# Residual stream with the tokens on the partitions in a four-layer pool, MLA, NA, pool backbone

## The chip, the cores and the metric

The kernel runs on one core of a Trainium2 chip. The metric is the device time of one execution in microseconds (us). A core has TensorE (PE; its weight loads are a row of their own, PEld), VectorE (DVE), ScalarE (ACT), GpSimd (POOL) and SyncE (SP), which here issues DMAs.

## The reference, cut to what matters

Two streams, 256 latent tokens `x` and 256 context tokens `ctx`, have 1024 channels and pass four layers. A layer has a token mixer (pool, MLA, NA, pool) and a SwiGLU FFN of 2816 hidden channels. Shift, scale and gate of each half come from `silu(c) @ ada_w[i]` (1024 by 6144, fp32, one map of weights for both streams).

```
for i in range(4):
    h = rmsnorm(x, norm_g[i, 0]) * (1 + sc_m) + sh_m
    x = x + g_m * rmsnorm(mixer(h), norm_g[i, 1])
    h = rmsnorm(x, norm_g[i, 2]) * (1 + sc_f) + sh_f
    x = x + g_f * rmsnorm((silu(h @ wg) * (h @ wu)) @ w_down, norm_g[i, 3])
```

The context does the same in layers 0 and 1 with its own shift, scale and gate. In layer 2 it only gives keys and values, and layer 3 has the latent tokens alone. The pool mixer takes, for four groups of 256 channels, the mean over a centred window of 2, 4, 8 or 16 tokens less the token itself, times a 256 by 256 matrix for each group and a scale for each channel.

## The kernel before, in words

Every value that goes into a large product is split into two fp32r parts, hi and lo, and a product is three matmuls: hi hi, hi lo, lo hi (`mm3`, L332 to L337). Weights come from DRAM as chunks of eight 128 by 128 tiles (512 KB, five `raw` slots). ACT makes hi (L157), DVE makes lo (L161), five chunks of each are kept, and each chunk is used once.

The residual stream `xs` has channels on the partitions: eight tiles of 128 channels by 512 tokens, latent tokens first. In all products the weights are stationary and the tokens move, 512 columns where both streams pass (layers 0 and 1) and 256 where the latent tokens pass alone. An output product (`ffn_down`, `Wo.rest`) makes one tile of 128 output channels after another. Since a norm runs over the channels, its sums go across partitions: for each tile `y_stats` (L495 to L512) makes squares and a product on ACT and DVE, POOL adds them to a running sum (L512), and at the end PE sums over the partitions (L526), ACT and DVE make the factors, and PE spreads them (L551). DVE and POOL then add to x (`post`, L571, L573), and `renorm` (L600, L589, L591) makes the two parts of the next h, tile by tile.

What lies between two sub-layers is called an edge here: from the first matmul of an output product's last part to the end of `head` (L910 to L913), which multiplies h with the first four column tiles of the next weights as h comes. The order in an edge is written by hand, one letter a step (`ORDERS`, read by `Edge.run`). With both streams the last four column tiles are made for the latent tokens first and for the context (`quanta`) while the latent h is made. The letters p and q prepare weights, the letter a is a step of the adaLN maps on PE: four fp32 matmuls with one 512 KB chunk of `ada_w` (L379), of which a unit (one of six of a layer) has eight. All other adaLN steps are done by DVE in the FFNs (L395).

The first layer's pool mixer (`start`) takes window sums with DVE and POOL adds along the tokens; the last layer's (`pool`) multiplies with a 256 by 256 band matrix for each group. `Closing` ends the program: transposes of x and of the gated y, the norm, and four stores.

## Time and profile before

| | us |
|---|---|
| median of 3 runs (1777.34 to 1782.39) | 1780.4 |
| span of the profiled execution, first to last instruction | 1779.5 |
| PE busy | 1676.0 |
| DVE busy | 1177.7 |
| ACT busy | 726.8 |
| POOL busy | 248.4 |

The profile gives the profiled execution's span and no device time of its own for it; the span lies within the range of the three runs. A share of busy time is a mean over stages. The matmuls' ends are modelled and overlap, so a busy PE says little by itself; the distance from one matmul's start to the next is what counts.

### The profile page before, as it was taken

To read this page: it belongs to the slowest core of one execution; us is meant where nothing else is said; L and a number is where in the kernel's file an instruction comes from. 1 tells how busy PE (TensorE), PEld (TensorE's weight loads), DVE (VectorE), ACT (ScalarE), POOL (GpSimd) and SP (SyncE) were. 2 spreads that over 40 slices of the span, in tenths; PEclk is the share of its full clock that TensorE was granted. 3 is DMA by queue.
4 is the path that set the end of the run, shared out by engine and by line. 5 is a ranking of instruction groups with operands and counts; after the bars stand their busy time and mean duration, and the time that the engine had idled before them with its cause. 6 is when DMAs were issued, how large, how long until landed. Compare 5 with 4: busy or idle time off the path is not lost.

```text
span 1779.5 us, 27077 instructions
## 1 busy us (share of the span) xinstructions
PE 1676.0 (94%) x10726; PEld 1453.7 (82%) x10726; DVE 1177.7 (66%) x1833; ACT 726.8 (41%) x1264; POOL 248.4 (14%) x199
## 2 busy tenths in 40 slices
PE   4789999999999999899999999899989999989998
...
GB/s 303 288 184 219 170 197 172 156 175 160 48 99 43 43 123 56 48 211 180 191 176 168 176 154 55 127 91 114 114 131 203 304 285 190 190 93 203 181 186 73
DMA packets 82270, 279.45 MB, mean 157 GB/s; under 512 B 9312, under 2 KB 16224, under 8 KB 82144
## 3 DMA queue, kind: packets, MB, share of 16 engines
...
q8 instruction: 84, 1.38, 0.3%
q10 hardware_dynamic: 1568, 0.86, 0.2%
...
HBM read 276.65 MB, written 1.05 MB: 156 GB/s over the span
## 4 chain that ended last, share of the span: by engine, by line
PE 82%; DVE 11%; ACT 4%; issue 1%; DMA 1%; POOL 0%; ACTq 0%; DVEq 0%; POOLq 0%
PE acc L335 21%; PE acc L336 21%; PE acc L337 21%; PE acc L913 2%; PE acc L910 2%; PE acc L911 2%; PE adp L379 2%; PE aux L335 2%; DVE wl L161 2%; PE aux L336 2%; PE aux L337 1%; DMA raw<-in_ada_w 1%; DVE yq L507 1%; DVE rh L591 1%; PE aux L1484 1%
## 5 line engine op out<-in xcount | busy, mean ns | idle before, releaser
L161 DVE TENSOR_TENSOR wl<-raw,wh 128x1024 fp32r<-128x1024 f32 x323 | 408.5, 1271 | 218.6 <-ACT wh L157 215.6
L335 PE MATMUL acc<-rh,wh 128*128 128x256 f32 (+1 forms) x1392 | 468.9, 337 | 0.0
L336 PE MATMUL acc<-rh,wh 128*128 128x256 f32 (+1 forms) x1392 | 465.3, 334 | 2.3 <-DVE rh L350 2.3
L337 PE MATMUL acc<-rh,wl 128*128 128x256 f32 (+1 forms) x1392 | 465.0, 334 | 0.0
L157 ACT ACTIVATE wh<-raw 128x1024 fp32r<-128x1024 f32 x323 | 337.1, 1051 | 237.9 <-PE acc L336 121.0
L512 POOL TENSOR_TENSOR ya<-ya,yq 128x768 f32<-128x768 f32 x71 | 146.6, 2070 | 1081.3 <-DVE yq L507 715.2
L335 PEld LDWEIGHTS acc<-rh,wh 128*128 128x128 f32 x1392 | 265.2, 191 | 34.4 <-issue 7.4
L336 PEld LDWEIGHTS acc<-rh,wh 128*128 128x128 f32 x1392 | 265.4, 191 | 27.5 <-DVE rh L350 2.5
L337 PEld LDWEIGHTS acc<-rh,wl 128*128 128x128 f32 x1392 | 265.2, 191 | 26.3 <-DVE wl L161 0.2
L335 PE MATMUL acc<-rx,wh 128*128 128x256 f32 (+1 forms) x816 | 260.8, 320 | 0.0
L337 PE MATMUL acc<-rx,wl 128*128 128x256 f32 (+1 forms) x816 | 259.1, 318 | 0.0
L336 PE MATMUL acc<-rx,wh 128*128 128x256 f32 (+1 forms) x816 | 259.1, 317 | 0.0
L395 DVE SCALAR_TENSOR_TENSOR ff_a<-raw,sc,ff_a 128x1024 f32<-128x1024 f32 x154 | 192.1, 1278 | 0.6 <-DMA raw<-in_ada_w 0.3
L335 PEld LDWEIGHTS acc<-rx,wh 128*128 128x128 f32 x816 | 154.5, 189 | 12.0 <-issue 0.8
L337 PEld LDWEIGHTS acc<-rx,wl 128*128 128x128 f32 x816 | 154.4, 189 | 11.3
L336 PEld LDWEIGHTS acc<-rx,wh 128*128 128x128 f32 x816 | 154.6, 189 | 11.1
L364 ACT ACTIVATE rx<-big 128x512 fp32r<-128x512 f32 (+1 forms) x80 | 42.0, 525 | 247.3 <-DVE big L681 247.3
L681 DVE TENSOR_TENSOR big<-big,acc 128x512 f32<-128x512 f32 (+1 forms) x88 | 48.6, 552 | 112.4 <-PE acc L337 107.8
L910 PE MATMUL acc<-rh,wh 128*128 128x256 f32 x304 | 85.9, 310 | 8.0 <-ACT rh L589 6.8
L589 ACT ACTIVATE rh<-t,m 128x256 fp32r<-128x256 f32 x88 | 44.9, 510 | 108.5 <-DVE t L600 108.4
L911 PE MATMUL acc<-rh,wl 128*128 128x256 f32 x304 | 83.3, 301 | 0.0
L350 DVE TENSOR_TENSOR rx<-big,rx 128x512 fp32r<-128x512 f32 (+1 forms) x80 | 44.7, 559 | 47.3 <-ACT rx L364 47.3
...
## 6 DMA issues: line engine op xcount, KB each, us to landing
raw<-in_ada_w SPq DMA_DIRECT2D x192, 512.0 KB, 4.6
raw<-in_gu SPq DMA_DIRECT2D x176, 512.0 KB, 4.3
raw<-in_dn SPq DMA_DIRECT2D x88, 512.0 KB, 4.2
raw<-in_nwin SPq DMA_DIRECT2D x24, 512.0 KB, 3.6
raw<-in_mwo SPq DMA_DIRECT2D x8, 512.0 KB, 3.8
raw<-in_nwo SPq DMA_DIRECT2D x8, 512.0 KB, 3.7
raw<-in_mwin SPq DMA_DIRECT2D x6, 512.0 KB, 3.6
...
```

The costliest lines, as they stand in the source:

```text
L157: nc.scalar.activation(out=hi[:, 0:n, :], in_=raw, func=AF.Copy)
L161: nc.vector.tensor_tensor(out=lo[:, 0:n, :], in0=raw, in1=hi[:, 0:n, :].bitcast(F32), op=ALU.subtract)
L335: nc.tensor.matmul(out, wh, ah, start=start, stop=False)
L336: nc.tensor.matmul(out, wh, al, start=False, stop=False)
L337: nc.tensor.matmul(out, wl, ah, start=False, stop=stop)
L350: self.nc.vector.tensor_tensor(out=lo, in0=src, in1=hi.bitcast(F32), op=ALU.subtract)
L395: nc.vector.scalar_tensor_tensor(out=acc[:, i, :], in0=v, scalar=c, in1=acc[:, i, :], op0=ALU.mult, op1=ALU.add)
L512: (eng or nc.gpsimd).tensor_tensor(out=st[key], in0=st[key], in1=q, op=ALU.add)
L589: nc.scalar.activation(out=hi, in_=t, func=AF.Identity, bias=b)
L681: nc.vector.tensor_tensor(out=b, in0=b, in1=psu[:, sl], op=ALU.mult)
L910: n.nc.tensor.matmul(ps[c][:, sl], wh, hi, start=(k == 0), stop=False)
L911: n.nc.tensor.matmul(ps[c][:, sl], wl, hi, start=False, stop=False)
```

## The change

The residual stream becomes `xt`, four tiles of 128 tokens by 1024 channels. Output products take the two parts of the activations as stationary operand, 128 tokens at a time, and the weights as moving operand, 512 output channels at a time (`mm3t`, `down`, `Wo.product`); the weights are packed anew on the host for this. Norms are sums along a row: ACT squares with an accumulated sum, then a mean, a root and a reciprocal of one column (`factor`). The gate, times the norm's gain, is a row: `ada_steps` keeps it as `row`, and `gates` copies it to all partitions with four DMAs a stream from POOL's queue. h is made from the normalised rows by PE transposes, then scale and shift per channel (`make_h`). Both pool mixers are products with the band matrix (`mix`), and the first layer's channel scale goes into the weights. `Closing`, `y_stats`, `y_sums`, `renorm` and the letters of the edges are gone. In an edge, tasks with dependencies, a priority and an assumed duration are put in order by `Sched`, while the program is built; the engines then run in that fixed order. The attentions, the FFNs' first products and the letters inside the attentions stay.

A sub-layer's last part now makes the first 512 channels of all its token tiles, then the other 512 tile by tile (`Edge.second`); with more than ten k tiles the second part is begun with the first ones (`k0`). The adaLN steps that the letter a put into the edges are done elsewhere: all 40 of the first layer's first five units in `arrive`, one unit (layer 3, shift of the FFN) in a row by `need`, the rest by DVE.

```diff
-    def ffn_down(self, l, two, base, nk, d, sl):
-        a = self.acc()
-        for k in range(nk):
-            hi, lo = self.hid_slot(two, k)
-            act = (hi[:, sl], lo[:, sl]) if two else (hi, lo)
-            self.mm3(a[:, sl], self.w(f"dn{l}", base + d * nk + k), act, k == 0, k == nk - 1)
-        return a
...
-    def y_stats(self, st, l, i, s, d, key="acc", eng=None):
...
-        q = self.p["bd"].tile([128, 3, 256], F32, tag="ya" if first else "yq", name="ya" if first else "yq", bufs=2 if first else 3)
-        nc.scalar.activation(out=q[:, 0, :], in_=y, func=AF.Square)
-        nc.vector.scalar_tensor_tensor(out=q[:, 1, :], in0=y, scalar=g, in1=x, op0=ALU.mult, op1=ALU.mult)
-        nc.scalar.activation(out=q[:, 2, :], in_=y, func=AF.Square, scale=g)
-        if first:
-            st[key] = q
-        else:
-            (eng or nc.gpsimd).tensor_tensor(out=st[key], in0=st[key], in1=q, op=ALU.add)
...
-        for d in range(KT - tail):
-            a = n.ffn_down(l, two, base, nk, d, full)
-            if not last:
-                evac(a, d, full)
-                continue
-            if d:
-                close.turn_y(d - 1)
-            close.evac(a, d)
-        for d in range(KT - tail, KT):
...
+    def mm3t(self, out, act, wt, start, stop):
+        nc = self.nc
+        (wh, wl), (ah, al) = wt, act
+        nc.tensor.matmul(out, ah, wh, start=start, stop=False)
+        nc.tensor.matmul(out, ah, wl, start=False, stop=False)
+        nc.tensor.matmul(out, al, wh, start=False, stop=stop)
...
+    def ada_steps(self, l, u):
...
+            row = self.row[key]
+            nc.vector.tensor_tensor(out=row, in0=ps, in1=gc[:, 0, :], op=ALU.add)
+            yield
+            nc.vector.tensor_tensor(out=row, in0=row, in1=gc[:, 1, :], op=ALU.mult)
+            yield True
+            return
...
+    def gates(self, l, u, name, streams, eng):
...
+        def load(s):
+            for i in range(4):
+                r = self.row[key][32 * i + s:32 * i + s + 1, :]
+                eng.dma_start(out=g[:, s, 256 * i:256 * i + 256], in_=r.unsqueeze(1).to_broadcast([1, 128, 256]))
...
+    def down(self, a, t, two, name, tile, hid, start, stop):
+        wh, wl = self.w(name, tile, 4)
+        hi, lo = self.hid_slot(two, hid)
+        self.mm3t(a, [v[:, 128 * t:128 * t + 128] for v in (hi, lo)], (wh, wl), start, stop)
...
+class Sched:
+    HOP = 0.15
+    SLACK = 0.25
...
+    def run(self):
...
+        while left:
+            can = {}
+            for i, t in left:
+                if any(d.end is None for d in t.deps) or any(o.start is None for o in t.order):
+                    continue
+                at = max([t.ready] + [o.start for o in t.order])
+                options = []
+                for e, dur in t.eng.items():
+                    s = max([at, free[e]] + [d.end + (self.HOP if d.on != e else 0) for d in t.deps])
+                    options.append((s + dur, s, e))
+                end, s, e = min(options)
+                can.setdefault(e, []).append((s, t.prio, i, t, end))
+            best = None
+            for e, c in can.items():
+                m = min(x[0] for x in c)
+                x = min((x for x in c if x[0] <= m + self.SLACK), key=lambda x: (x[1], x[2]))
+                if best is None or x[0] < best[0][0]:
+                    best = x, e
+            (s, _, i, t, end), e = best
+            t.start, t.end, t.on = s, end, e
+            free[e] = end
+            t.fn(e) if len(t.eng) > 1 else t.fn()
+            left = [x for x in left if x[0] != i]
...
+class Edge:
...
+    def second(self, nk, product, begun=None, k0=0):
+        n, s = self.n, self.s
+        use = [[] for _ in range((nk - k0) // 2)]
+        for i, t in enumerate(self.tiles):
+            tag = "acc"
+            slot = self.slot(tag)
+            if begun:
+                slot.tile = begun[t]
+            last = None
+            for k in range(k0, nk):
+                def go(t=t, k=k, slot=slot, tag=tag):
+                    if slot.tile is None:
+                        slot.tile = getattr(n, tag)()
+                    product(slot.tile, t, k)
+                new = slot if not begun and k == k0 else None
+                last = s.add({"P": 0.69}, go, [last], 4, new=new, slots=() if new else (slot,))
+                use[(k - k0) // 2].append(last)
+            self.parts[t, 1] = [lambda slot=slot: slot.tile, [last], slot]
+        self.chunks += use
+        self.have = len(self.chunks)
+    def factor(self, t, c, k, deps, prio):
+        n = self.n
+        v, m, r = self.cols(t, c, k), self.cols(t, c + k, 1), self.cols(t, c + k + 1, 1)
+        def mean():
+            j = n.small("j4", 4)[:, 0:k]
+            n.nc.vector.tensor_scalar(out=j, in0=v, scalar1=1.0 / D, scalar2=0.0, op0=ALU.mult, op1=ALU.add, accum_out=m)
+        a = self.s.add({"D": 0.15}, mean, deps, prio)
+        a = self.s.add({"A": 0.2}, lambda: n.nc.scalar.activation(out=r, in_=m, func=AF.Sqrt, bias=n.eps), [a], prio)
+        return self.s.add({"D": 0.08}, lambda: n.nc.vector.reciprocal(out=r, in_=r), [a], prio), r
...
+    def chain(self, close=False):
+        n, s, nc = self.n, self.s, self.n.nc
+        i = 1 if self.u == 2 else 3
+        G, load = n.gates(self.l, self.u, f"G{self.l}_{self.u}", len(self.streams), nc.gpsimd)
+        loads = {}
+        for c in self.streams:
+            if self.gate:
+                loads[c] = s.add({"A": 0.4}, lambda c=c: load(c), self.gate, 2)
+            else:
+                load(c)
+        for t in self.tiles:
+            prio = 1 + t // 2 * 1.5
+            c = t // 2
+            gdeps, gready = ([loads[c]], 0.0) if self.gate else ([], 3.0)
+            done, sqs = {}, []
+            for h in range(2):
+                ps, made, slot, *ends = self.parts[t, h]
+                y, hs = n.Y[2 * t + h], slice(512 * h, 512 * h + 512)
+                p = prio
+                if self.fold:
+                    def add(y=y, ps=ps):
+                        nc.vector.tensor_tensor(out=y, in0=ps(), in1=y, op=ALU.add)
+                    f = s.add({"D": 0.69}, add, made, p, slots=(slot,))
+                    def sq(y=y, t=t, h=h):
+                        nc.scalar.activation(out=n.small("junk", 512, 1), in_=y, func=AF.Square, accum_out=self.cols(t, 4 + h, 1))
+                    q = s.add({"A": 0.56}, sq, [f], p)
+                    sqs.append(q)
+                    def gy(y=y, hs=hs, c=c):
+                        nc.vector.tensor_tensor(out=y, in0=y, in1=G[:, c, hs], op=ALU.mult)
+                    done[h] = s.add({"D": 0.56}, gy, [f, q] + gdeps, p, ready=gready)
+                    continue
+                gs = [(slice(0, 512), None)] if not ends else [(slice(256 * e, 256 * e + 256), 2 * h + e) for e in range(2)]
+                ys = []
+                for e, (sl, g) in enumerate(gs):
+                    end = None if g is None else n.edge[:, t % 2, g:g + 1]
+                    def sq(ps=ps, sl=sl, end=end, t=t, col=4 + (h if g is None else g)):
+                        k = dict(scale=end) if end is not None else {}
+                        nc.scalar.activation(out=n.small("junk", 512, 1)[:, sl], in_=ps()[:, sl], func=AF.Square, accum_out=self.cols(t, col, 1), **k)
+                    sqs.append(s.add({"A": 0.6 if g is None else 0.42}, sq, made, p, slots=(slot,)))
+                    def gy(y=y, ps=ps, sl=sl, end=end, c=c, h=h):
+                        o, q, k = y[:, sl], ps()[:, sl], G[:, c, 512 * h + sl.start:512 * h + sl.stop]
+                        if end is None:
+                            nc.vector.tensor_tensor(out=o, in0=q, in1=k, op=ALU.mult)
+                        else:
+                            nc.vector.scalar_tensor_tensor(out=o, in0=q, scalar=end, in1=k, op0=ALU.mult, op1=ALU.mult)
+                    ys.append(s.add({"D": 0.69 if g is None else 0.42}, gy, made + gdeps, p, slots=(slot,), ready=gready))
+                done[h] = ys[-1]
+                self.parts[t, h] = None
+            fac, r = self.factor(t, 4, len(sqs), sqs, prio)
+            new = {}
+            for h in range(2):
+                def up(t=t, h=h, r=r):
+                    x = n.xt[:, t, 512 * h:512 * h + 512]
+                    nc.vector.scalar_tensor_tensor(out=x, in0=n.Y[2 * t + h], scalar=r, in1=x, op0=ALU.mult, op1=ALU.add)
+                    if close:
+                        (nc.scalar if h else nc.sync).dma_start(out=n.out[128 * t:128 * t + 128, 512 * h:512 * h + 512], in_=x)
+                new[h] = s.add({"D": 0.69}, up, [fac, done[h]], prio)
+            if not close:
+                self.normed(t, new, prio)
...
+    def make_h(self, l, i):
+        n, s, nc = self.n, self.s, self.n.nc
+        if not self.end_units:
...
+                    def turn(t=t, dp=dp, slot=slot, xs=xs):
+                        if slot.tile is None:
+                            slot.tile = n.aux()
+                        for e in range(2):
+                            j = 128 * (2 * dp + e) % 512
+                            o = 256 * e + 128 * (t % 2)
+                            nc.tensor.transpose(slot.tile[:, o:o + 128], xs.tile[:, j:j + 128], n.ident)
...
+                    def high(slot=slot, e=e, hi=hi, a=a, b=b):
+                        nc.scalar.activation(out=hi, in_=slot.tile[:, 256 * e:256 * e + 256], func=AF.Identity, scale=a, bias=b)
+                    def whole(slot=slot, e=e, tmp=tmp, a=a, b=b):
+                        tmp.tile = n.small("t")
+                        nc.vector.tensor_scalar(out=tmp.tile, in0=slot.tile[:, 256 * e:256 * e + 256], scalar1=a, scalar2=b, op0=ALU.mult, op1=ALU.add)
+                    def low(tmp=tmp, hi=hi, lo=lo):
+                        nc.vector.tensor_tensor(out=lo, in0=tmp.tile, in1=hi.bitcast(F32), op=ALU.subtract)
+                    w = s.add({"D": 0.4}, whole, trs + units, prio, new=tmp, slots=(slot,))
+                    q = s.add({"A": 0.46}, high, trs + units, prio, slots=(slot,))
+                    self.hs[c, d] = [s.add({"D": 0.36}, low, [w, q], prio, slots=(tmp,)), q]
...
+        def product(a, t, h, k, base=base, nk=nk):
+            n.down(a, t, two, name, base + 4 * (h * nk + k), k, k == 0, k == nk - 1)
...
+        ps = [n.acc() for _ in tiles]
+        for k in range(nk):
+            for t in tiles:
+                product(ps[t], t, 0, k)
+        k0 = max(0, nk - 2 * W_BUFS)
+        begun = [n.acc() for _ in tiles] if k0 else None
+        for k in range(k0):
+            for t in tiles:
+                product(begun[t], t, 1, k)
+        edge = Edge(n, l, 5, tiles)
+        edge.fold = si > 0
+        for t in tiles:
+            edge.first(t, ps[t], "acc")
+        edge.second(nk, lambda a, t, k: product(a, t, 1, k), begun, k0)
+    if last:
```

DVE between FFN 0 and MLA, in the middle of the edge. `y` is the output, `a` and `xx` the sums, `t` what goes to h. Before:

```order
L1014 TENSOR_TENSOR y_104<-acc,y_104 128x256
L507 SCALAR_TENSOR_TENSOR yq<-y_104,mod_154,xs 128x256
L543 TENSOR_SCALAR a_3753<-aux 128x6
L546 RECIPROCAL rs_3754<-rs_3754 128x2
L559 SCALAR_TENSOR_TENSOR a_3753<-a_3753,rs_3754 128x1 x2
L559 SCALAR_TENSOR_TENSOR xx<-a_3753,rs_3754,xx 128x1 x2
L562 TENSOR_SCALAR xx<-xx 128x2
L565 RECIPROCAL rs_3755<-rs_3755 128x2
L161 TENSOR_TENSOR wl<-raw,wh 128x1024
L1014 TENSOR_TENSOR y_105<-acc,y_105 128x256
L507 SCALAR_TENSOR_TENSOR yq<-y_105,mod_154,xs 128x256
L571 SCALAR_TENSOR_TENSOR t<-y_100,mod_154,aux 128x256
```

and now (`G` is the gate's row on all partitions, `st` the sums of a row):

```order
L825 TENSOR_TENSOR y_102<-y_102,G_5_3456 128x512
L825 TENSOR_TENSOR y_104<-y_104,G_5_3456 128x512
L160 TENSOR_TENSOR wl<-raw,wh 128x1024
L816 TENSOR_TENSOR y_99<-acc,y_99 128x512
L825 TENSOR_TENSOR y_99<-y_99,G_5_3456 128x512
L764 TENSOR_SCALAR j_3535,st<-st 128x2
L767 RECIPROCAL st<-st 128x1
L852 SCALAR_TENSOR_TENSOR xt<-y_98,st,xt 128x512
L852 SCALAR_TENSOR_TENSOR xt<-y_99,st,xt 128x512
L764 TENSOR_SCALAR j_3557,st<-st 128x2
L767 RECIPROCAL st<-st 128x1
L786 TENSOR_SCALAR big<-xt,st 128x512
```

The tile-by-tile sums and the chain of two-column instructions are gone; a token tile's norm is a few instructions between the products of the next tile, and half as many instructions are twice as long.

PE between FFN 2 and the last pool mixer. Before, one unit of the adaLN maps (`adp<-raw,sc`) stands in pieces behind the sums and between the mixer's products:

```order
L526 MATMUL aux<-ones,ya 128x1 x2
L551 MATMUL aux<-ident,rs_13954 128x128 x2
L379 MATMUL adp<-raw,sc 32x256 x4
L551 MATMUL aux<-ident,rs_13955 128x128 x2
L379 MATMUL adp<-raw,sc 32x256 x12
L728 MATMUL acc<-wh,rh 128x256
L729 MATMUL acc<-wl,rh 128x256
L730 MATMUL acc<-wh,rh 128x256
```

Now a whole unit, 32 matmuls, stands ahead of the last 20 steps of the output product:

```order
L358 MATMUL acc<-wh,rx_27_161 128x512
L359 MATMUL acc<-wl,rx_27_161 128x512
L360 MATMUL acc<-wh,rx_27_161 128x512
L402 MATMUL adp<-raw,sc 32x256 x32
L447 MATMUL adp<-ident,ada 128x128 x2
L358 MATMUL acc<-wh,rx_28_162 128x512
L359 MATMUL acc<-wl,rx_28_162 128x512
L360 MATMUL acc<-wh,rx_28_162 128x512
L358 MATMUL acc<-wh,rx_29_163 128x512
```

The unit moved from the waits of the edge to a place among products.

PE in the first layer. Before, the adaLN steps and the first pool products take turns:

```order
L379 MATMUL adp<-raw,sc 32x256 x20
L409 MATMUL adp<-ident,ada 128x128 x2
L379 MATMUL adp<-raw,sc 32x256 x32
L409 MATMUL adp<-ident,ada 128x128 x2
L379 MATMUL adp<-raw,sc 32x256 x16
L335 MATMUL acc<-rh,wh 128x256
L336 MATMUL acc<-rh,wh 128x256
L337 MATMUL acc<-rh,wl 128x256
```

Now one adaLN step stands among the latent tokens' 48 product and 32 window matmuls, the others behind the last of those (the first two rows here):

```order
L949 MATMUL acc<-rx_22_156,rx_35_169 128x256
L949 MATMUL acc<-rx_23_157,rx_35_169 128x256
L402 MATMUL adp<-raw,sc 32x256 x8
L881 MATMUL aux<-ident,big 128x128 x8
L402 MATMUL adp<-raw,sc 32x256 x32
L447 MATMUL adp<-ident,ada 128x128 x2
L402 MATMUL adp<-raw,sc 32x256 x12
L881 MATMUL aux<-ident,big 128x128 x4
```

Before, each group's twelve products were followed by adaLN steps; now the steps wait for the whole mixer.

## Rows read from the trace of the kernel before

**Rows 1.** The page's head.
```profile
span 1779.5 us, 27077 instructions
```

**Rows 2.** Windows, the seven edges: us, PE PEld DVE ACT POOL busy (x), PEclk, DMA, GB/s
```profile
0.00:132.30 132.30, 91.26 (x741) 60.20 (x741) 107.26 (x206) 54.29 (x114) 55.99 (x63) 0.85 0.75 259
...
426.00:522.20 96.20, 88.69 (x596) 82.96 (x595) 67.05 (x115) 38.29 (x70) 37.72 (x26) 0.95 0.22 72
...
673.60:756.90 83.30, 74.87 (x501) 70.69 (x499) 59.33 (x95) 38.50 (x79) 40.75 (x26) 0.92 0.16 51
...
1048.40:1140.20 91.80, 84.50 (x551) 76.79 (x553) 63.36 (x114) 35.99 (x69) 39.68 (x26) 0.94 0.24 72
...
1307.00:1354.30 47.30, 41.50 (x294) 40.38 (x295) 38.95 (x58) 27.22 (x49) 20.45 (x12) 0.86 0.30 93
...
1472.20:1592.00 119.80, 107.62 (x854) 101.14 (x853) 83.42 (x138) 61.19 (x105) 25.45 (x21) 0.91 0.49 154
...
1707.00:1779.50 72.50, 65.68 (x554) 65.36 (x552) 25.05 (x24) 27.38 (x39) 6.61 (x7) 0.97 0.38 118
```

**Rows 3.** Timeline of PE in FFN 0: twelve matmuls apart.
```profile
200.13 0.39 PE L336 MATMUL acc<-rh,wh 128*128 128x512 f32 x1
...
202.85 0.39 PE L336 MATMUL acc<-rh,wh 128*128 128x512 f32 x1
```

**Rows 4.** Windows, FFN 3, all matmuls 256 wide: columns as in Rows 2.
```profile
1600.00:1700.00 100.00, 100.00 (x836) 100.00 (x835) 58.00 (x71) 48.30 (x72) 0.00 (x0) 1.00 0.59 191
```

**Rows 5.** Groups by line and form, DVE: count, busy us, mean ns, idle before.
```profile
L161 DVE TENSOR_TENSOR wl<-raw,wh 128x1024 fp32r<-128x1024 f32 x322 | 407.8, 1273 | 218.6 <-ACT wh L157 215.6 <-PE aux L489 1.9
...
L681 DVE TENSOR_TENSOR big<-big,acc 128x512 f32<-128x512 f32 x44 | 30.2, 686 | 93.8 <-PE acc L337 90.8 <-ACT big L680 2.9
...
L571 DVE SCALAR_TENSOR_TENSOR t<-y,mod,aux 128x256 f32<-128x256 f32 x56 | 26.3, 469 | 0.5 <-PE aux L551 0.5
...
L1161 DVE TENSOR_SCALAR big<-big,rc 128x512 f32<-128x512 f32 x38 | 18.5, 487 | 1.3
...
L562 DVE TENSOR_SCALAR xx<-xx 128x2 f32<-128x2 f32 x11 | 3.4, 309 | 0.3
...
L546 DVE RECIPROCAL rs<-rs 128x2 f32<-128x2 f32 x11 | 1.8, 162 | 2.9 <-ACT rs L544 2.9
```

**Rows 6.** Groups by line and form, ACT.
```profile
L157 ACT ACTIVATE wh<-raw 128x1024 fp32r<-128x1024 f32 x322 | 336.5, 1053 | 237.9 <-PE acc L336 121.0 <-issue 65.8 <-DMA raw<-in_gu 23.5
...
L364 ACT ACTIVATE rx<-big 128x512 fp32r<-128x512 f32 x40 | 25.3, 632 | 176.5 <-DVE big L681 176.5
...
L1151 ACT ACTIVATION_READ_ACCUMULATOR big<-big,mx 128x1 f32 x64 | 11.9, 187 | 0.0
...
L942 ACT ACTIVATE y<-acc,mod 128x256 f32<-128x256 f32 x8 | 3.8, 470 | 0.0
...
L544 ACT ACTIVATE rs<-a,eps 128x2 f32<-128x2 f32 x11 | 3.3, 296 | 21.6 <-DVE a L537 11.5 <-DVE a L543 10.0
```

**Rows 7.** The chain in order of time: start, us, what.
```profile
1229.88 0.87 PE acc L1533 x8
...
1299.08 1.00 PE adp L379 x16
```

**Rows 8.** Windows, a stretch of the start: columns as in Rows 2.
```profile
11.20:16.30 5.10, 4.49 (x32) 2.50 (x31) 2.70 (x6) 2.01 (x6) 4.27 (x7) 1.00 1.02 406
```

**Rows 9.** DMA issues on the page: count, KB each, us to landing.
```profile
raw<-in_ada_w SPq DMA_DIRECT2D x192, 512.0 KB, 4.6
```

**Rows 10.** Timeline between FFN 1 and NA: POOL and DVE at once.
```profile
1105.24 1.84 POOL L512 TENSOR_TENSOR ya<-ya,yq 128x768 f32<-128x768 f32 x1 [0.56 <-ACT yq L508]
...
1105.28 2.08 DVE L591 SCALAR_TENSOR_TENSOR rh<-t,m,rh 128x256 fp32r<-128x256 f32 x1
```

**Rows 11.** The tile rh's instructions on DVE, 426 to 522: ns minimum/median/maximum.
```profile
L591 DVE SCALAR_TENSOR_TENSOR rh<-t,m,rh x16: 471/480/2061, 484.3 to 518.7; 128x256 fp32r<-128x256 f32 x16
```

**Rows 12.** Timeline of the last microseconds.
```profile
1773.90 1.26 POOL L967 TENSOR_TENSOR xs<-big,xs 128x512 f32<-128x512 f32 x1 [9.35 <-ACT big L966]
```

More of the change, by code (lines that the diff above doesn't have):

```diff
@@ L381, in products @@
             on = 1
+        gate = u in (2, 5)
+        if gate:
+            gc = self.p["tmp"].tile([128, 2, 256], F32, tag="gc", name="gc", bufs=1)
+            nc.sync.dma_start(out=gc, in_=self.ins["gate"][l, u // 3])
         for k in range(KT):
@@ new lines, in pool, with start, __init__ @@
+    edge.chain()
+    edge.make_h(l, 0)
+    edge.mix(l, lambda g, k: n.R[4 + 2 * g + k][:, 256:512])
+    return edge
+def start(n):
+    n.region("rx0")
+    n.space("bds")
+    n.table(AF.Sqrt)
+    edge = Edge(n, 0, None, range(4))
+    edge.arrive()
+    edge.make_h(0, 0)
+    edge.mix(0, lambda g, k: n.R[32 + g][:, 256 * k:256 * k + 256])
+    return edge
+class Task:
+    def __init__(self, eng, fn, deps, order, prio, ready):
+        self.eng, self.fn, self.deps, self.order, self.prio, self.ready = eng, fn, deps, order, prio, ready
+        self.start = self.end = None
@@ L976, in ffn @@
     segs = [12, 10] if two else [22]
-    sty = [{}, {}]
     full = slice(0, 512) if two else slice(0, 256)
-    close = Closing(n, l, 3) if last else None
-    ps = edge.run(ORDERS["f" + str(l)], f"gu{l}", turn=close and close.turn_x)
+    tiles = range(4) if two else range(2)
+    edge.chain()
+    edge.make_h(l, 2)
+    ps = edge.head(f"gu{l}")
     if l == 0:
-        n.region("rx0")
+        n.late_consts()
     n.space(f"ff{l}")
     if l == 2:
-        nc.sync.dma_start(out=n.xs[:, :, 256:512], in_=n.ins["band"])
+        nc.sync.dma_start(out=n.xt[:, 2:4, :].rearrange("p a b -> p (a b)"), in_=n.ins["band"].rearrange("p a b -> p (a b)"))
+        n.load_pool_s(1)
     n.rate = RATE[l]
@@ L1034, in ffn @@
     if last:
-        return close.run()
-    return Edge(n, l, 3, (l + 1, 0), sty, quanta)
+        edge.chain(True)
+        edge.run()
+    return edge
 def run(gen):
@@ L1190, in evac_a @@
                 n.stat_add(stq[s], ps[:, n.sl(s)])
-    ps = edge.run(ORDERS["b1"], "mwin")
+    edge.chain()
+    edge.make_h(l, 0)
+    ps = edge.head("mwin")
     n.space("pt1")
@@ L1562, in split_o @@
         return go()
-    ps = edge.run(ORDERS["b2"], "nwin", (2, 3))
+    edge.chain()
+    edge.make_h(l, 0)
+    ps = edge.head("nwin", (2, 3))
     for e in range(2):
@@ L1599, in na @@
     n.space("bdn")
-    sty = [{}, {}]
-    for d in range(KT):
-        a = ahead.rest(d, lat)
-        nc.scalar.activation(out=Y[d][:, 0:256], in_=a[:, 0:256], func=AF.Copy)
-        n.y_stats(sty[0], l, 1, 0, d, "acc" if d < KT - 1 else "last")
-    return Edge(n, l, 1, (l, 2), sty)
+    return ahead.rest(l, 2)
 def pack(w, order):
```

780 lines of the change are left out of this document (334 added, 446 removed).

## The prediction

> **What bounds the kernel now.** I read the span first [rows 1]: 1779.5 us of the profiled execution, 0.9 under the median of 1780.4 and within the range of the three runs; what lies around the span has no row, so I take the sum's difference off the median. Then the timeline of PE inside an FFN. Twelve matmuls with 512 moving columns start 2.72 us apart, 0.227 each [rows 3]; with 256 columns, 836 start in 100 us, 0.120 each [rows 4]. The FFNs and attentions run at this pace and stay as they are. What the change touches are seven edges, which I measured as stretches between a first and a last matmul [rows 2]: 132.3, 96.2, 83.3, 91.8, 47.3, 119.8 and 72.5 us, together 643.2. The reader is to see that PE is not full there, that its mean clock is 0.85 to 0.97, and that POOL, idle in the FFNs, works for up to 41 us in an edge.
>
> **Removed, added, and the cost of each.** First the matmuls that an edge needs after the change, by the order of instructions. For two streams an output product of ten k tiles is 10 x 4 token tiles x 2 halves x 3 = 240 matmuls of 512: 54.5 us. The first head is 192 of 256: 23.0. Transposes: 32 at 0.87 for eight [rows 7], 3.5.
> - FFN 0 to MLA: 54.5 + 23.0 + 3.5 = 81.0, against 96.2 now.
> - MLA to FFN 1: 52 of 64 k steps are left after those begun in the attention, 156 matmuls, 35.4; 35.4 + 23.0 + 3.5 = 61.9, against 83.3.
> - FFN 1 to NA: the context has half a head, 144 matmuls, 17.3; in all 75.3, against 91.8.
> - NA to FFN 2: 60 matmuls of 512 (13.6), head 96 of 256 (11.5), transposes 1.7: 26.8, against 47.3.
> - FFN 2 to FFN 3: 22 x 2 x 2 x 3 = 264 of 512: 59.9 (before 528 of 256 at 0.120: 63.4, so moving weights alone give 3.5 us here and 3.5 at the end, and nothing where 512 tokens moved already). Pool products 48 (5.8) and windows 32 (3.8) of 256, transposes 3.5, head 11.5, and the adaLN unit: 32 matmuls at 1.00 for sixteen [rows 7], 2.0. Together 86.5, against 119.8.
> - End: 59.9, against 72.5.
>
> Second, the chain that each token tile goes through when its last product is done, in durations of like instructions [rows 5, 6]: sum with the first segment 0.69, square with its accumulator read 0.63 + 0.19, mean 0.31, root 0.30, reciprocal 0.16, x += 0.69, square 0.82, mean, root and reciprocal 0.77, scale 0.49, two transposes 0.22, the whole h 0.47, its low part 0.47: 6.2 us. The second half row queues behind the first once at the update and once at the scale, 1.2 more: 7.4. No add of POOL stands in it. What it replaces held POOL adds, sums, spreads and a second chain for x.
>
> Where does it lie? With two streams the latent tiles are done first and their chains lie beside the products of the context tiles, 2 x 30 matmuls, 13.6 us. The context's chain lies beside the latent head, 11.5 us; but the context's eight h tiles need 8 x 0.94 = 7.5 us of DVE, which comes late by 7.4 + 7.5 - 11.5 = 3.4, and the latent transposes wait in PE's order too. I take 5 us of stalls in each of the three two-stream edges (bounds 0 and 12). The clock: 4% to 8% of these edges are lost now after idle time [rows 2]; with half the stalls I leave 2. The weight's 512 columns may also move a little slower than tokens; no row shows them, so 1 to 1.6 more (bounds 0 and 2). That is 89.6, 71 (one for the gate's DMAs behind the attention's buffers) and 85.4 (1.5 more, since the context's half head of 5.8 us is shorter than its 7.5 us of DVE): gains of 6.6, 12.3 and 6.4.
>
> NA to FFN 2 has one stream, so nothing covers the chain of the second tile: 13.6 + 7.4 + 11.5 + the transposes ahead, 1.8. The clock is at its lower level for (1 - 0.86) x 2 x 47.3 = 13 us there now [rows 2], and an idle stretch of some 8 us stays, so 4. Two for queueing on DVE: 40.5, a gain of 6.8.
>
> FFN 2 to FFN 3 has such a chain twice. 86.5 + 7.4 to the mixer + 3 for the split between pool products and windows + 7.4 to the head + 4 of clock + 5 of queueing. And the adaLN unit that now stands in a row ahead of the last 20 products: five `raw` slots hold its first five chunks, the last three can only be asked for when PE has used the first ones, 4.6 us to landing [rows 9] and 1.3 between chunks (512 KB at the 406 GB/s of a full stretch [rows 8]), 6 us in which PE, and behind it ACT and DVE, wait. Before, these steps stood in PE's idle time. 119.3: no gain.
>
> End: 59.9 + square, mean, root, reciprocal, update (2.3) + hops 0.5 + what follows the last result now, 1779.5 - 1775.2 = 4.3 [rows 1, 12]: 67, a gain of 5.5.
>
> The start is bound by DMA. 40 adaLN and 6 weight chunks at 1.29 are 59 us, x and band some 6, and the first chunk lands at 10: 75 if slots never run out. They do: 80 product and window matmuls of the latent tokens (9.6 us) stand on PE with one adaLN step among them, and the low parts of the pool's weights (1.27 each, [rows 5]) stand on DVE behind the h tiles, so their slots come free late. With 6 and 8 us of standing loads the last unit is there at 92, the context's mixing ends at about 106, its chain and h at 122, its head at 134: 1.7 worse than 132.3 (bounds 116, if the loads never stand, and 142).
>
> **Sum.** 134 + 89.6 + 71 + 85.4 + 40.5 + 119.3 + 67 = 606.8 for 643.2; 36.4 off 1780.4 is 1744. With all stalls at nothing and the start at 116 it would be about 1680, with all at their upper bounds about 1795.
>
> [...] In one place DVE's split of h took 2.08 us while POOL's add took 1.84 beside it [rows 10], and the same form took 0.48 in the median of another edge, 2.06 at most [rows 11]. So I price the new chain at the undisturbed durations. [...]
>
> **Rivals.**
> - Nearly all stalls close and the start's loads hardly stand: 3 us less in each two-stream edge, 10 in FFN 2 to FFN 3, 12 in the start: 1744 - 31 = 1713. For it: the last h tile needs 0.94 us, less than the head's 1.44 a step. Against it: orders found with assumed durations below the rows (a square 0.58 against 0.82, a root 0.20 against 0.30).
> - Most is eaten: loads stand to the upper bound (start 142) and the order makes weights of the head wait behind chain work, 5 us in each two-stream edge and 4 in the others: 1744 + 8 + 19 = 1771 or a little more.
> - The gate's rows are late. They come by DMAs from POOL's queue, which the trace has none of; the nearest row is 4.6 us for 512 KB. After NA only 2.7 us of products lie ahead of them: 3 us there, 5 in the start: 1752. [...]
> - The other side: DVE becomes the bound of the edges. In the second half of a two-stream edge it has for each tile 2.76 of sums and gates, 0.47 of mean and reciprocal, 1.38 of updates, 0.47 and half of 0.98: 5.6, times four 22.3; 16 x 0.94 of h; seven low parts of 1.27: 46 us in 54 us of PE. If its instructions were a fifth dearer than their rows, it is full: 9 us for each of three edges, 3, 6 and 10 for the others: 1790. It decides from about 18% on. Against it: what made DVE dear is POOL, and POOL has no adds left in the edges.
>
> **How the numbers follow.** Forecast (1730 to 1765, late gates included) 0.53, first rival 0.16, second 0.17, the last 0.14. A measurement of this kernel tells 0.3%, 5 us, from no change. Of the second rival about half lies under 1775: faster 0.53 + 0.16 + 0.08 = 0.77; same 0.09; slower 0.14. The range 1712 to 1786 leaves out some 0.07 below and 0.13 above.
>
> **What would show it.** Per edge: no POOL adds; DVE's split of h at 0.43 to 0.48 throughout; PE's stalls of 5, 7 to 8 and twice 8 us; a hole of 6 us around the adaLN block in FFN 2 to FFN 3; the start ending near 134. Wrong would be: a pitch of moving weights well over 0.227, a start of 120 or of 145, or holes in front of the head's weights.

## The result and the profile after

The changed kernel takes 1790.76 us (median of 4 runs, 1789.17 to 1791.52), the kernel before 1779.49 beside it: a ratio of 1.0063, 95% interval 1.0049 to 1.0078. It is slower by 0.6%. The forecast was 1744 with a range to 1786: the time lies outside, on the other side of no change.

The first lines to read are the page's span, the queue of POOL (packets, MB, and the time its packets took as a share of 16 engines' span), and the DMA issues by group (count, KB each, median us to landing).

```profile
span 1788.7 us, 24745 instructions
...
q0 software_dynamic: 2304, 6.29, 7.4%
...
raw<-in_ada_w SPq DMA_DIRECT2D x192, 512.0 KB, 4.7
...
G<-row POOLq DMA_DIRECT2D x48, 128.0 KB, 19.1
```

A 512 KB chunk lands 4.7 us after its issue, a gate copy of a quarter of that in 19.1; much of that is time behind the copies ahead of it, since the first of a group lands after 6.7 to 8.3 us and the next ones up to 5.7 us apart. The copies move 6.29 MB of 289.76 and take 7.4% of the engines' span, 132 us of all sixteen. Then the seven edges as windows of the changed kernel, with the columns of [rows 2].

```profile
0.00:160.30 160.30, 93.30 (x745) 64.59 (x746) 67.91 (x167) 62.58 (x144) 4.57 (x12) 0.79 0.69 210
...
452.60:538.30 85.70, 82.44 (x466) 71.42 (x466) 49.90 (x99) 38.66 (x76) 0.00 (x0) 1.00 0.43 91
...
689.30:765.30 76.00, 67.84 (x395) 59.12 (x394) 41.20 (x89) 36.27 (x75) 4.30 (x8) 0.98 0.48 77
...
1054.80:1136.30 81.50, 78.25 (x421) 67.07 (x424) 50.73 (x101) 40.47 (x80) 0.00 (x0) 0.98 0.43 90
...
1302.50:1350.90 48.40, 31.59 (x182) 27.48 (x181) 25.07 (x49) 23.38 (x46) 2.12 (x4) 0.82 0.59 113
...
1468.80:1606.10 137.30, 105.58 (x543) 85.36 (x541) 67.83 (x118) 57.18 (x104) 1.50 (x3) 0.81 0.54 145
...
1721.90:1788.70 66.80, 60.05 (x266) 49.40 (x264) 28.70 (x34) 24.00 (x31) 0.00 (x0) 0.99 0.39 129
```

| edge | before | forecast | after | off by |
|---|---|---|---|---|
| start | 132.3 | 134 | 160.3 | +26.3 |
| FFN 0 to MLA | 96.2 | 89.6 | 85.7 | -3.9 |
| MLA to FFN 1 | 83.3 | 71 | 76.0 | +5.0 |
| FFN 1 to NA | 91.8 | 85.4 | 81.5 | -3.9 |
| NA to FFN 2 | 47.3 | 40.5 | 48.4 | +7.9 |
| FFN 2 to FFN 3 | 119.8 | 119.3 | 137.3 | +18.0 |
| end | 72.5 | 67 | 66.8 | -0.2 |

Four edges are shorter than before; the start and FFN 2 to FFN 3 lose 45.5 between them. Outside the edges the span has 1132.7 us for 1136.3. What PE waits for in the start is in its timeline (start, us, instruction, and in brackets the idle time before it and what ended it):

```profile
80.09 1.08 PE L402 MATMUL adp<-raw,sc 128*32 128x256 f32 x8 [9.18 <-DMA raw<-in_ada_w]
...
95.69 1.08 PE L402 MATMUL adp<-raw,sc 128*32 128x256 f32 x8 [11.83 <-DMA raw<-in_ada_w]
```

and what DVE waits for at the same time:

```profile
74.71 0.48 DVE L843 SCALAR_TENSOR_TENSOR y<-acc,edge,G 128x256 f32<-128x256 f32 x1 [7.04 <-DMA G<-row]
79.58 0.48 DVE L843 SCALAR_TENSOR_TENSOR y<-acc,edge,G 128x256 f32<-128x256 f32 x1 [4.39 <-DMA G<-row]
85.32 0.48 DVE L843 SCALAR_TENSOR_TENSOR y<-acc,edge,G 128x256 f32<-128x256 f32 x1 [5.25 <-DMA G<-row]
89.96 0.48 DVE L843 SCALAR_TENSOR_TENSOR y<-acc,edge,G 128x256 f32<-128x256 f32 x1 [4.16 <-DMA G<-row]
```

DVE waits for gates from MLA to FFN 1 and from NA to FFN 2 too; the longest wait of each:

```profile
715.08 0.69 DVE L841 TENSOR_TENSOR y<-acc,G 128x512 f32<-128x512 f32 x1 [9.15 <-DMA G<-row]
...
1322.00 0.69 DVE L841 TENSOR_TENSOR y<-acc,G 128x512 f32<-128x512 f32 x1 [6.53 <-DMA G<-row]
```

In the start the waits of the two engines have one possible source. Two windows, one of a stretch without copies and one of the 29.5 us from the first copy's issue to the last one's landing, show what the DMA engines do (the last two columns are the DMA engines' share and GB/s):

```profile
11.20:16.30 5.10, 3.64 (x44) 1.42 (x36) 0.00 (x0) 0.09 (x1) 0.00 (x0) 1.00 1.03 410
66.80:96.30 29.50, 5.25 (x64) 1.39 (x56) 4.62 (x11) 2.67 (x7) 4.38 (x8) 0.62 0.99 163
```

The engines are as busy as when they move 410 GB/s, and move 163. So the copies may cost twice: the gates come late, and adaLN and weight chunks stand behind them. FFN 2 to FFN 3 has two holes. While the copies issued from 1466 to 1470 are under way (the last lands at 1494.73), the down weights come late: a weight split of ACT waits 14.53 us, and PE 4.79 behind it. Later the adaLN unit waits for its last chunks:

```profile
1494.51 1.06 ACT L156 ACTIVATE wh<-raw 128x1024 fp32r<-128x1024 f32 x1 [14.53 <-DMA raw<-in_dn]
```

```profile
1495.62 0.80 PE L358 MATMUL acc<-wh,rx 128*128 128x512 f32 x1 [4.79 <-ACT wh L156]
```

```profile
1528.29 1.08 PE L402 MATMUL adp<-raw,sc 128*32 128x256 f32 x8 [3.27 <-DMA raw<-in_ada_w]
1530.08 1.08 PE L402 MATMUL adp<-raw,sc 128*32 128x256 f32 x8 [0.70 <-DMA raw<-in_ada_w]
1531.61 1.08 PE L402 MATMUL adp<-raw,sc 128*32 128x256 f32 x8 [0.45 <-DMA raw<-in_ada_w]
```

### The profile page after: what moved, and what is told of

Same layout as the page of the kernel before. It is cut to its first block, busy times and chain, and to the rows that moved or that the text cites. A ratio compares the mean times of both kernels' runs of the same rounds, so it can differ in the third digit from the quotient of the medians.

```text
span 1788.7 us, 24745 instructions
## 1 busy us (share of the span) xinstructions
PE 1637.7 (92%) x9662; PEld 1379.4 (77%) x9662; DVE 1088.4 (61%) x1763; ACT 725.8 (41%) x1285; POOL 47.6 (3%) x70
## 2 busy tenths in 40 slices
DMA packets 83780, 289.76 MB, mean 162 GB/s; under 512 B 10192, under 2 KB 13008, under 8 KB 83536
## 3 DMA queue, kind: packets, MB, share of 16 engines
q0 software_dynamic: 2304, 6.29, 7.4%
## 4 chain that ended last, share of the span: by engine, by line
PE 77%; DMA 8%; DVE 8%; ACT 4%; issue 1%; POOL 0%; DVEq 0%; ACTq 0%; SPq 0%
PE acc L350 13%; PE acc L351 13%; PE acc L352 13%; PE acc L358 6%; PE acc L359 6%; PE acc L360 6%; DMA raw<-in_ada_w 4%; DMA G<-row 2%; PE adp L402 2%; PE acc L981 2%; PE acc L980 2%; PE acc L983 2%; DMA raw<-in_dn 1%; PE aux L350 1%; DVE t L895 1%
## 5 line engine op out<-in xcount | busy, mean ns | idle before, releaser
L350 PE MATMUL acc<-rh,wh 128*128 128x512 f32 (+1 forms) x1296 | 439.0, 339 | 0.0
L351 PE MATMUL acc<-rh,wh 128*128 128x512 f32 (+1 forms) x1296 | 436.6, 337 | 0.0
L352 PE MATMUL acc<-rh,wl 128*128 128x512 f32 (+1 forms) x1296 | 436.5, 337 | 0.0
L350 PEld LDWEIGHTS acc<-rh,wh 128*128 128x128 f32 x1296 | 245.9, 190 | 30.5 <-issue 3.7
L351 PEld LDWEIGHTS acc<-rh,wh 128*128 128x128 f32 x1296 | 246.1, 190 | 25.0
L358 PE MATMUL acc<-wh,rx 128*128 128x512 f32 x528 | 209.2, 396 | 4.8 <-ACT wh L156 4.8
L359 PE MATMUL acc<-wl,rx 128*128 128x512 f32 x528 | 207.5, 393 | 0.5 <-DVE wl L160 0.5
L360 PE MATMUL acc<-wh,rx 128*128 128x512 f32 x528 | 207.2, 392 | 0.0
L358 PEld LDWEIGHTS acc<-wh,rx 128*128 128x128 f32 x528 | 100.5, 190 | 25.7 <-ACT wh L156 5.2
L359 PEld LDWEIGHTS acc<-wl,rx 128*128 128x128 f32 x528 | 100.4, 190 | 21.5 <-DVE wl L160 1.0
L360 PEld LDWEIGHTS acc<-wh,rx 128*128 128x128 f32 x528 | 100.2, 190 | 21.2
L402 PE MATMUL adp<-raw,sc 128*32 128x256 f32 x512 | 47.8, 473 | 58.3 <-DMA raw<-in_ada_w 57.8
L881 PE MATMUL aux<-ident,big 128*128 128x128 f32 x208 | 39.8, 325 | 49.3 <-DVE big L786 38.1
L881 PEld LDWEIGHTS aux<-ident,big 128*128 128x128 f32 x208 | 27.4, 164 | 63.5 <-DVE big L786 41.0
## 6 DMA issues: line engine op xcount, KB each, us to landing
G<-row POOLq DMA_DIRECT2D x48, 128.0 KB, 19.1
```

Of the source, the lines that this page charges most:

```text
L350: nc.tensor.matmul(out, wh, ah, start=start, stop=False)
L351: nc.tensor.matmul(out, wh, al, start=False, stop=False)
L352: nc.tensor.matmul(out, wl, ah, start=False, stop=stop)
L358: nc.tensor.matmul(out, ah, wh, start=start, stop=False)
L359: nc.tensor.matmul(out, ah, wl, start=False, stop=False)
L360: nc.tensor.matmul(out, al, wh, start=False, stop=stop)
```

## The experiments

Stages below run from the end of one head to the end of the next, read on PE's timeline of one execution; a stage holds what lies between two edges and the edge at its end, and bears that edge's name. Starts with the same instructions ended 5 us apart in two profiles (160.3 in the changed kernel, 155.0 in the second run below), so a difference of less than that is not read from a start. In a later stage two runs with the same instructions on PE, DVE and ACT differ by up to 1.5 (to NA, gates_by_dram and dram_pieces).

| run | start | to MLA | to FFN 1 | to NA | to FFN 2 | to FFN 3 | rest | time | ratio to before, 95% |
|---|---|---|---|---|---|---|---|---|---|
| before | 132.3 | 389.9 | 234.7 | 383.3 | 214.1 | 237.7 | 187.5 | 1779.5 | |
| changed | 160.3 | 378.0 | 227.0 | 371.0 | 214.6 | 255.2 | 182.6 | 1790.8 | 1.0049 to 1.0078 |
| gates_by_pe | 147.1 | 381.6 | 225.1 | 373.1 | 214.8 | 252.2 | 184.9 | 1780.7 | 0.9998 to 1.0017 |
| unit_by_dve | 155.0 | 381.2 | 226.9 | 371.2 | 214.7 | 241.0 | 182.6 | 1777.4 | 0.9978 to 0.9998 |
| gates_pe_unit_dve | 148.8 | 384.3 | 225.4 | 372.7 | 214.6 | 238.6 | 185.0 | 1771.1 | 0.9939 to 0.9969 |
| gates_act_queue | 158.2 | 398.6 | 240.5 | 392.7 | 217.3 | 261.7 | 190.5 | 1862.4 | 1.0456 to 1.0487 |
| gates_by_dram | 144.9 | 378.1 | 221.1 | 369.6 | 206.6 | 245.2 | 182.6 | 1750.0 | 0.9821 to 0.9850 |
| dram_unit_dve | 142.3 | 379.7 | 222.8 | 372.7 | 207.4 | 234.8 | 182.6 | 1743.7 | 0.9790 to 0.9820 |
| dram_unit_dve_ada_first | 138.6 | 379.7 | 221.3 | 371.2 | 206.4 | 234.6 | 182.6 | 1736.3 | 0.9745 to 0.9778 |
| dram_pieces | 142.7 | 378.0 | 221.4 | 371.1 | 206.5 | 245.2 | 182.6 | 1749.3 | 0.9825 to 0.9852 |
| dram_and_idle_copies | 158.2 | 378.0 | 223.2 | 371.0 | 211.0 | 254.8 | 182.6 | 1780.8 | 1.0006 to 1.0024 |
| best_slack | 147.0 | 383.5 | 221.5 | 374.7 | 206.9 | 235.1 | 182.6 | 1749.6 | 0.9828 to 0.9855 |
| copies_alternated | 152.5 | 378.0 | 222.9 | 371.1 | 210.3 | 245.0 | 182.6 | 1764.4 | 0.9899 to 0.9932 |

**The copies away, by PE (gates_by_pe).**

```diff
-                eng.dma_start(out=g[:, s, 256 * i:256 * i + 256], in_=r.unsqueeze(1).to_broadcast([1, 128, 256]))
...
+        self.nc.tensor.matmul(ps, self.ident[:, j:j + 1].to_broadcast([128, 128]), self.row[key], start=True, stop=True)
...
+            self.nc.scalar.activation(out=g[:, s, 256 * i:256 * i + 256], in_=ps, func=AF.Copy)
```

> The gate rows are spread over the partitions by PE products with a column of the identity and an ACT copy, and no longer by 48 DMAs; the rest is the changed kernel. Theory 1 (the row copies fill the DMA engines for 20 to 30 us a time, so they hold up the adaLN and weight chunks and come late themselves): the start ends near 138 instead of 160.3, NA to FFN 2 takes 42 instead of 48.4, FFN 2 to FFN 3 takes 131 instead of 137.3, the others stay within 2; in all 1757 (1748 to 1766). Theory 2 (the order is what is wrong: a block of products ahead of adaLN steps at the start, and chains one behind the other): within 5 us of 1790.

1780.7: neither theory. The start came down by 13.2, not the 22 of theory 1; NA to FFN 2 did not gain, and FFN 2 to FFN 3 gained 3.0, not 6.3. The substitute has a price of its own. A pair of row products takes PE 1.13 us in the start, one pair after the other behind ACT's copies, and the adaLN steps, whose chunks are there, stand behind them:

```profile
67.92 1.13 PE L549 MATMUL adp<-row,ident 128*128 128x256 f32 x4 [0.75 <-ACT G L552]
69.80 1.13 PE L549 MATMUL adp<-row,ident 128*128 128x256 f32 x4 [0.53 <-ACT G L552]
71.68 1.13 PE L549 MATMUL adp<-row,ident 128*128 128x256 f32 x4 [0.53 <-ACT G L552]
73.56 2.37 PE L403 MATMUL adp<-raw,sc 128*32 128x256 f32 x40 [0.31 <-ACT G L552]
```

The stages to MLA and to NA became 3.6 and 2.1 longer. The run doesn't tell the theories apart; a cheaper substitute was needed.

**The queue (gates_act_queue).**

```diff
-        G, load = n.gates(self.l, self.u, f"G{self.l}_{self.u}", len(self.streams), nc.gpsimd)
+        G, load = n.gates(self.l, self.u, f"G{self.l}_{self.u}", len(self.streams), nc.scalar)
```

> The same 48 row copies, issued by ACT instead of POOL. If it is POOL's queue that makes them slow, eight copies land within 10 us of the first issue and the time is that of the spread by PE, about 1757. If it is the copy itself (one partition's row read 128 times), they take 20 to 30 us as before, and the time is 1785 to 1797.

1862.4, slower than any. POOL's queue is not the cause: from ACT's queue the start's eight copies still need 32.6 us from the first issue (66.44) to the last landing (99.04). Beyond the expectation, ACT itself now stands: it issues the eight over 20 us (the last at 86.48), where POOL took 4, and its next h part waits 13.75 us.

```profile
89.91 1.48 ACT L891 ACTIVATE rh<-aux,m,mod 128x256 fp32r<-128x256 f32 x3 [13.75 <-DMA G<-row]
```

**The adaLN unit (unit_by_dve, gates_pe_unit_dve).**

```diff
-RATE = (1.27, 1.27, 0.83, 0.5)
+RATE = (1.4, 1.27, 0.83, 0.5)
```

> DVE does ten more adaLN steps in FFN 0 (rate 1.40 for 1.27), so that the unit with the shift of layer 3's FFN no longer stands as 32 matmuls on PE ahead of the last 20 products of FFN 2. If the prediction's hole is what it was said to be, FFN 2 to FFN 3 falls from 137.3 by 8 to 11 (2 of matmuls, 5 of waiting for chunks, the clock after it), 1781 in all. If the weights behind the unit in the load queue were the wait, or the chain behind it takes up the slack, by less than 3.

1777.4, a gain of 13.4, more than expected. The stage to FFN 3 falls from 255.2 to 241.0. The hole was there and nearly of the size said: 5.1 us of PE's idle time between 1523 and 1535, 4.6 of them for chunks. The rest was larger. The trace has two records for each of the unit's fp32 products, 64 for 32, so by the price that the prediction took they cost 4.0 us where it counted 2.0. And the clock was granted at 0.70 in those 12 us: after the first wait a step of eight records takes 1.08 us (the rows above), at a granted clock of 0.50; the first four steps had taken 1.97 together, at 1.00. From the unit's first matmul to the next product it is 11.8 us, and the 15 us behind it still have 0.90.

> Both: gate rows by PE, and the adaLN unit by DVE in FFN 0 (rate 1.45). If the two losses are apart, their gains add: 1747 (1738 to 1757), with FFN 2 to FFN 3 near 121. If they are one and the same wait for chunks, no better than the better one of the two.

1771.1: a miss, with the cost of the row products in it (the stage to MLA is 6.3 longer than in the changed kernel, 3.6 with the row products alone, 3.2 with the unit alone). Beside the two measured gains, 10.0 and 13.4, it is 19.7, so they nearly add. The rate is 1.45 here.

**The same bytes from another source (gates_by_dram, dram_pieces).** When a gate row is made, a DMA of 4 KB for each stream puts it into DRAM; the copies to 128 partitions read it there.

```diff
+            for i in range(1 + two):
+                nc.gpsimd.dma_start(out=self.flat[key][i].rearrange("(a b) -> a b", a=4), in_=row[i:128:32, :])
...
-            for i in range(4):
-                r = self.row[key][32 * i + s:32 * i + s + 1, :]
-                eng.dma_start(out=g[:, s, 256 * i:256 * i + 256], in_=r.unsqueeze(1).to_broadcast([1, 128, 256]))
+            d = self.flat[key][s]
+            eng.dma_start(out=g[:, s, :], in_=d.partition_broadcast(128))
```

> The gate rows go to DRAM by two small DMAs when they are made, and are copied to the 128 partitions from there, by POOL's queue as before, with as many bytes written to SBUF. Theory 1a (all 16 engines reading the one partition that holds the row is what is slow): a stream's 512 KB lands some 3 us after its issue, the start ends near 141 (160.3), the wait ahead of the head from NA to FFN 2 falls from 19.0 to about 10.3 as with PE, and FFN 2 to FFN 3 loses its first hole of 5: 1757 (1750 to 1765), without the 4 us that the spread by PE put into each edge. Theory 1b (128 short writes, or POOL's queue, are what is slow): copies of 20 us again and 1785 or more.

1750.0, 40.7 less than the changed kernel. POOL's queue and the copies on this run's page:

```profile
q0 software_dynamic: 2112, 6.34, 1.1%
...
G<-flat POOLq DMA_DIRECT2D x12, 512.0 KB, 5.5
```

6.34 MB in 1.1% of the engines' span, for 7.4%. But rows of 4 KB took the place of rows of 1 KB, so size and source had changed together. The second run parts them (its edit against the first):

```diff
-            eng.dma_start(out=g[:, s, :], in_=d.partition_broadcast(128))
+            for i in range(4):
+                eng.dma_start(out=g[:, s, 256 * i:256 * i + 256], in_=d[256 * i:256 * i + 256].partition_broadcast(128))
```

> Gate rows from DRAM again, but in 48 copies of 128 KB with rows of 1 KB, as the changed kernel has them; only the source differs from it. If it is the one source partition that is slow, the copies land about as fast as the 512 KB ones and the time stays at 1750 (1746 to 1755). If short rows of 1 KB are a good part of it, the copies take 10 us and more and the time is over 1760.

```profile
G<-flat POOLq DMA_DIRECT2D x48, 128.0 KB, 4.7
```

1749.3: the same count, size and queue as in the changed kernel, 4.7 us to landing for 19.1. The source is the cause. POOL's queue, which these copies use as well, is cleared by the same line.

**Which partitions (copies_alternated).**

```diff
-            for i in range(4):
+            for i in (0, 2, 1, 3):
```

> The changed kernel with its 48 copies out of one partition, a stream's four in the order of partitions 0, 64, 32, 96 (plus the stream) instead of 0, 32, 64, 96. In the profile of the changed kernel eight copies take 29.5 us: the first four land some 5 us apart, the last four within 6.4 us, as if two groups of partitions had a path of their own each. If so, neighbours in the queue now use different paths, eight copies take about 20 us, and the time falls by 8 to 14 (1777 to 1783). If each copy has its price whatever partition it reads, 29 us again and 1788 to 1793.

1764.4, twice the gain expected, for an order of four. Eight copies take 24.2 us in the start, not 29.5 (43 GB/s for 36, at 1 MB), so which partitions are read one after the other matters; that fits two paths, one for 0 and 32 and one for 64 and 96, if not as far apart as the 20 expected. The gain is that of four stages: 7.8 in the start, 4.1 to FFN 1, 4.3 to FFN 2, and 10.2 to FFN 3, as much as rows from DRAM gave there. How a fifth off the copies' time does that stays open. No run reads the rows from more partitions, so it is not shown whether the few partitions or SBUF as a source make the copies slow; the two paths themselves are not shown either.

**Late or in the way (dram_and_idle_copies).** The edit is against gates_by_dram.

```diff
             eng.dma_start(out=g[:, s, :], in_=d.partition_broadcast(128))
+            for i in range(4):
+                r = self.row[key][32 * i + s:32 * i + s + 1, :]
+                eng.dma_start(out=spare[:, s, 256 * i:256 * i + 256], in_=r.unsqueeze(1).to_broadcast([1, 128, 256]))
```

> Gate rows come from DRAM as in the run of 1750, and behind them in the same queue the 48 copies out of the one partition are made as well, into a tile that nobody reads. It parts the loss of 41 us in two. If the copies cost by being late (the gates' products wait for them), the time stays near 1750. If they cost by holding the DMA engines while adaLN and weight chunks wait, most of the start's 15 and all of FFN 2 to FFN 3's 10 come back, the 8 of NA to FFN 2 do not: 1775 (1768 to 1785).

1780.8: with copies that nobody reads, 31 of the 41 us are back. By stages, 13.3 of the start's 15.4, 9.6 of the 10.0 to FFN 3, and, against the expectation, also 4.4 of the 8.0 to FFN 2. The first line is the start's longest wait of PE, again for a chunk; the second is a flaw of the experiment:

```profile
95.72 1.08 PE L403 MATMUL adp<-raw,sc 128*32 128x256 f32 x8 [11.59 <-DMA raw<-in_ada_w]
```

```profile
710.55 1.29 DVE L847 TENSOR_TENSOR y<-acc,G 128x512 f32<-128x512 f32 x2 [6.85 <-DMA G<-flat]
```

From 66 us to the end of the start, PE's waits for chunks add up to 28.7 us in the changed kernel, 7.2 with rows from DRAM and 21.9 here. The flaw: the real copy of a second stream stands behind idle ones in the same queue and lands some 20 to 24 us after its issue. Only from MLA to FFN 1 did DVE wait for one, and that stage is 2.1 longer than with rows from DRAM, so at least 28.7 of the 30.8 are not a late gate. The queue's line shows both kinds of copies, twice the bytes in hardly more time than the one kind had taken:

```profile
q0 software_dynamic: 4416, 12.64, 7.5%
...
G_s<-row POOLq DMA_DIRECT2D x48, 128.0 KB, 19.1
```

**Both causes out, then the start's order (dram_unit_dve, dram_unit_dve_ada_first).** The first is gates_by_dram with the rate of unit_by_dve. The second changes one number more, the priority of an adaLN step in `arrive`:

```diff
-                t = s.add({"P": 0.45}, lambda: n.fill(1), last, 2, before["u", u, k], when["u", u, k])
+                t = s.add({"P": 0.45}, lambda: n.fill(1), last, 1, before["u", u, k], when["u", u, k])
```

> The same with the adaLN unit done by DVE in FFN 0 (rate 1.40). The unit alone was worth 13 us, 14 of them from FFN 2 to FFN 3. If that is apart from the copies, 1744 (1736 to 1752), and FFN 2 to FFN 3 is near 118; if part of it was the copies' hold on the weight chunks, some 5 less of a gain: 1749.

> The same again, and in the start an adaLN step goes ahead of the pool products as soon as its chunk is there (priority 1 instead of 2), so that the raw slots come free. The prediction priced loads that stand behind the block of products at 6 and 8 us. If so, the start ends 8 to 14 earlier than in the run without it, some 1734 in all. If the start is bound by the chain from the latent tokens' products through the gates to h, by less than 3, or it gets longer by the adaLN matmuls that now lie in front (5 us).

1743.7 and 1736.3. The unit gives 6.3 here: 10.4 in the stage to FFN 3, for 14.2 beside the slow copies, and 6.4 go again in the three stages from the start's end to NA. Of these, the 1.6 to MLA is there in the next run as well; the 1.7 and 3.1 of the other two are 0.2 and 1.6 there, near what equal instructions differ by. With the steps ahead of the pool products, PE's waits for chunks after 66 us fall from 8.6 to 0.8, so the loads did stand. By the medians that is worth 7.4, half of the 14 that the prediction gave them; the profiles show 3.7 of it in the start, and the rest lies in later stages, whose instructions are the same in the same order. 1736.3 is 2.4% less than before, the fastest of the runs. Windows of three of its stages, the start, NA to FFN 2 and FFN 2 to FFN 3:

```profile
0.00:138.60 138.60, 96.23 (x745) 66.73 (x746) 67.98 (x167) 62.26 (x144) 2.55 (x8) 0.83 0.67 243
...
1110.80:1317.20 206.40, 195.00 (x1363) 168.76 (x1360) 134.43 (x325) 106.72 (x209) 0.53 (x1) 0.98 0.39 127
1317.20:1551.80 234.60, 212.36 (x1464) 197.30 (x1463) 161.34 (x229) 116.14 (x198) 1.65 (x3) 0.93 0.64 215
```

**The order's slack (best_slack).** The edit is against dram_unit_dve_ada_first.

```diff
-    SLACK = 0.25
+    SLACK = 0.6
```

> The run of 1736 with the order's slack at 0.6 us instead of 0.25: an engine waits up to that long for a task of higher priority, so that on DVE fewer low parts of weights stand inside a token tile's chain, where one cost 0.7 us before a reciprocal. The prediction named orders found with too short durations as a cause of waits. If the chains of the one-stream edges gain, 1736 falls by 3 to 6; if the low parts then come late for the head, it stays or rises by as much.

1749.6, 13 more: a miss. The one-stream edges stay (206.9, 235.1), and the start, FFN 0 to MLA and FFN 1 to NA get 8.4, 3.8 and 3.5 longer. Waiting for tasks of the chain won nothing where the chain lies open, and why the start loses by it stays open.

## Why the prediction was wrong

**The step that failed is the price of the gate's DMAs.** The prediction named them as a rival (3 us after NA, 5 in the start, 1752) and took the price from the nearest row, 4.6 us for 512 KB [rows 9], a load from DRAM into all partitions. The copies read one partition at a time, and no row of before shows such a source. It was the rate that failed: 1 MB took 29.5 us, 36 GB/s, not the 406 of [rows 8]. Between the changed kernel and the run with the DRAM source lie 40.7 us, five times the 8 that the rival gave. The nearest row was taken as the value, with no bound above it; the bound was open.

**A second mechanism was missing altogether.** All the rival said was that gates, coming by DMAs from POOL's queue, are late; from the same queue copies out of DRAM landed in 4.7 us. Some 29 to 31 of the 41 us came from copies in the way of other loads, also in FFN 2 to FFN 3, where nobody waited for a gate.

**The other steps.**
- The pitch of moving weights: right. In the last edge the 264 products run from 1721.92 to 1781.9, 0.227 each, so nothing of the extra 1 to 1.6 for moving weights.

```profile
1721.92 0.40 PE L358 MATMUL acc<-wh,rx 128*128 128x512 f32 x1
1722.15 0.40 PE L359 MATMUL acc<-wl,rx 128*128 128x512 f32 x1
1722.39 0.39 PE L360 MATMUL acc<-wh,rx 128*128 128x512 f32 x1
```

- Two-stream edges: 85.7 and 81.5 for 89.6 and 85.4. PE is idle for 3.3 us in each where 5 was taken, and the clock stays at 1.00 and 0.98. MLA to FFN 1 was off by 5.0, and DVE waited 9.15 there for a gate; with rows from DRAM its stage fell by 5.9.
- DVE undisturbed: right. The split of h took 424 to 427 ns in all sixteen cases of FFN 0 to MLA, and DVE is busy for 49.9 of 85.7 us. The rival that was to end slower, DVE as the bound, did not occur; the sign came from elsewhere.

```profile
L898 DVE TENSOR_TENSOR rh<-t,rh x16: 424/425/427, 501.6 to 529.7; 128x256 fp32r<-128x256 f32 x16
```

- The chain after the last product: from the last product to the head's first one NA to FFN 2 has 19.0 us in the changed kernel (1317.87 to 1336.90) and 10.3 with rows from DRAM (1295.20 to 1305.48), for 7.4 and 1.8 of transposes. Right to about 1 us once the gates are there; the stage was forecast at 207.3 and is 206.6.
- The adaLN block: the hole was right (5.1 for 6, 4.7 with rows from DRAM), its sum too small: 14.2 of the stage for 8, or 10.4 with rows from DRAM. Its products were counted at half their records, 2.0 for 4.0, and the clock in it not at all. PE had the first four chunks without a wait, where five were counted.
- The start: standing loads were right in kind and at most half in size, 7.4 for 14. With rows from DRAM, unit and order it still ends at 138.6, above 134; with the slow copies, 160.3, it lies above the upper bound of 142 as well.
- The end: right, 66.8 for 67.
- Two slips that change nothing: the terms of NA to FFN 2 add up to 40.3, not 40.5, and POOL works up to 56 us in an edge (the start in [rows 2]), not 41.

That gates from DRAM and the unit by DVE give 1743.7 beside the forecast of 1744 is partly chance, since the forecast held the unit's 8 us in FFN 2 to FFN 3 and a start of 134, not 142.3.
